# One layer of a hybrid attention / gated DeltaNet trunk: the later tiles of the input projection issued in another order

## The chip, the cores and the metric

The kernel runs on one NeuronCore of a Trainium2 chip. The core has five engines with a queue each, and each queue is worked off in order: TensorE (PE in the profile; PEld is its weight load), VectorE (DVE), ScalarE (ACT), GpSimd (POOL) and SyncE (SP), which here issues the DMAs. The metric is device time in microseconds (us) from one launch, lower is better. Times below are from the hardware profiler or from the runs without it.

## The reference

A layer maps `x` of 1024 tokens by 1024 features to the same shape, in float32. Only the first of its three sub-layers (mixer, cross-attention to 256 memory tokens, SwiGLU) is touched:

```python
h = _rms_norm(x, g_mix_pre[l])
proj = h @ w_in[l]
aq, ak, av, dqkv, dgate, dalpha, dbeta = jnp.split(proj, IN_SPLITS, axis=-1)
aq = _rope(aq.reshape(b, s, ATTN_HEADS, ATTN_HEAD_DIM), positions)
ak = _rope(ak.reshape(b, s, ATTN_KV_HEADS, ATTN_HEAD_DIM), positions)
attn_o = _window_attention(aq, ak, av, attn_sink[l])            # +-128 tokens, 8 heads, 2 KV heads
dn_o = _gated_deltanet(dqkv, dgate, dalpha, dbeta, ...)         # 4 heads, two directions
mix = jnp.concatenate([attn_o, dn_o], axis=-1) @ w_out[l]
x = x + _rms_norm(mix, g_mix_post[l])
```

The DeltaNet part solves, in chunks, a unit lower triangular system for each head and direction and then scans over the chunks; at its end the output is multiplied by `silu(gate)`:

```python
sol = lax.linalg.triangular_solve(tmat, rhs, left_side=True, lower=True, unit_diagonal=True)
_, o = lax.scan(step, state0, xs)
o = o * jax.nn.silu(gate.astype(jnp.float32).reshape(b, s, DN_HEADS, DN_HEAD_V))
```

## The kernel before

Float32 products are built from a rounded high part and the rest (`split`, lines 102 and 103: ACT casts, DVE or POOL subtracts), three matmuls for each product. The normalised input `hT` stays in SBUF, transposed, in two halves of 512 tokens. A tile of the input projection is 128 of the 2832 columns: `load_w` (line 125 issues the DMA) loads and splits its weights, `proj` takes two PSUM banks from the pool `pg` (three banks), and `gemm_b` (line 260) does 24 matmuls of 512 columns for each half. "Half tile" below means these 24 matmuls.

The program issues tiles and other steps by three lists. A letter is a kind of step, a digit its tile or head:

- `ORDER_1`: D (projection and convolution of a DeltaNet head's q, k, v), P (prep: chunk products for a head), B (`base_inverse` for two heads: a forward substitution of 32 by 32 blocks, 30 rounds of two DVE operations at lines 510 and 512, begun by line 501 and ended by line 514; it reads `d_u` from DRAM at line 495 and stores to `d_inv` at line 519).
- `ORDER_2`, the one that is edited: G (`gate_proj`: ACT evicts each half with Silu, line 736, and SP stores it to `d_gate`, line 737), L (`levels` of a head: fetches the base inverses at line 530, copies at 540 to 553, then builds the inverse of the whole chunk from PE products at 569 and 575, with short DVE and ACT operations between, and stores it at 594), A (`attn_proj`: DVE evicts each half twice, lines 709 and 710, four DMAs rotate it, line 714, POOL adds, line 715, SP stores to `d_q` or `d_k`, line 716), V (`value_proj`, tile to `d_v`), W (`next_windows`: starts two attention windows and finishes the ones before).
- `ORDER_3`: M (memory norm), s01 (a step of both scans), W, K and V (keys and values of the memory). The scans' PE products are at line 763; they need the levels of all heads, and in their second half the gates, loaded from `d_gate`. Key products are at 891, value products at 907.

There are 16 windows (8 token blocks for 2 KV heads). One loads `kr`, `qr` and `vr`, splits them (lines 616 to 625, ACT and POOL), multiplies scores (633), reduces them on DVE (635), takes Exp on ACT (642 and 646), scales (650), transposes on PE (656), splits, and multiplies by the values (661). `kr`, `qr`, `vr` and the value bank have one buffer each.

What order do the engines run? The lists are not the queue order. A scheduler that plays the program through on a model of time (`schedule_with_timeline_sim=True`) deals out the instructions to the engines: of those that are ready in its model, the one that the program issues first goes first; weight loads go 300 places ahead (`AHEAD`). The result is fixed when the kernel is compiled, and the engines then keep to it. So an entry of a list sets a step's priority, and steps of later entries fill what earlier ones leave free.

After the scans come the output projection (`mid_gemm`, PE at line 991), cross-attention and the feed-forward part (from line 1072 on), which the lists do not touch.

Of the kernel before, what the change touches and what calls it, by code (L numbers as in the profile page):

```python
# [33 lines left out]


ORDER_1 = "D0 P0 D1 P1 D2 P2 D3 P3 B0 B1".split()
ORDER_2 = "G0 G1 G2 G3 L0 L1 V A4 A0 A1 W L2 L3 W W A2 A3 W".split()
ORDER_3 = ("M " + "s01 W K " * 5 + "s01 K " * 3 + "s01 V V").split()


# [35 lines left out]
def tile_hybrid_block(  # L76
# [11 lines left out]
    if dump is None:  # L88
        def dump(name, ap):
            pass  # L90
# [597 lines left out]
    def issue(order, table):  # L688
        for o in order:
            table[o[0]](*(int(c) for c in o[1:]))  # L690
# [47 lines left out]

    issue(ORDER_2, {"A": attn_proj, "V": value_proj, "G": gate_proj, "L": levels, "W": next_windows})
    dump("d_q", d_q); dump("d_k", d_k); dump("d_gate", d_gate); dump("d_v", d_v)  # L740
# [752 lines left out]
```

## Time and profile before

| what | value |
|---|---|
| median of 3 runs | 1596.54 us (1593.78 to 1598.5) |
| the profiled execution | 1601.45 us |
| its span, first to last instruction | 1599.7 us |
| mean granted clock of TensorE | 0.983 |
| stretch from the first gate tile to the output projection | 211.67 to 607.84 us |

The profiled execution is one run, with its own time; 1.75 us of it lie outside the span. In the profile a line `L260 PE MATMUL pg<-hhi,whi` is a matmul issued by line 260 of the kernel that writes the tile `pg` from `hhi` and `whi`. A wait row reads: engine, tile and line that waited, what released it, then the sum in us, how often, the longest. In a timeline row the first two numbers are start and duration. A busy share near one says that an engine had something in work, not that it worked at its full rate: the granted clock stands beside it.

### The profile page before, as it was taken

Reading aid. Unit: us, or ns where it says so; the run is one execution under the profiler, and the core shown is the slowest. Engines: PE = TensorE matmul, PEld = TensorE weight load, DVE = VectorE, ACT = ScalarE, POOL = GpSimd, SP = SyncE. Lnnn points to the kernel's source line nnn. Section 1 sums busy time; section 2 is a strip of 40 time slices with the busy share of each in tenths; the row PEclk is TensorE's granted clock in tenths of the full one; section 3 lists DMA queues with packets and bytes.
Section 4 is the critical chain, followed back from the end, with each engine's and each line's share of the span. In section 5 each row is a group of like instructions: output and inputs, shape, how many; then the busy total and the mean of one; then the engine's idle time right before and its main releaser. Section 6 shows DMA issues by size and latency. Waiting matters only on the chain. (4 is left out here: it accounts for less than half of the span.)

```text
span 1599.7 us, 21414 instructions
## 1 busy us (share of the span) xinstructions
PE 1523.6 (95%) x7558; PEld 1274.7 (80%) x7558; DVE 1034.0 (65%) x1596; ACT 766.2 (48%) x1561; POOL 522.8 (33%) x479
## 2 busy tenths in 40 slices
PE   6999889988899989999999999999999999999998
PEld 5877778877799967788888777778888888888786
DVE  6846886967677765454345549778765555587575
ACT  6566543326957785564334566223322323344532
POOL 2367653234335610243301140335433433100021
PEclk9999999998999999999999999999999999999999
DMA  6134258474999675354222254444333333763344
GB/s 205 41 109 124 59 159 239 129 192 122 296 324 277 193 266 191 145 185 152 73 69 80 90 185 139 150 157 152 100 120 118 104 99 99 272 222 108 110 169 160
DMA packets 265400, 247.29 MB, mean 155 GB/s; under 512 B 43960, under 2 KB 200525, under 8 KB 265293
## 3 DMA queue, kind: packets, MB, share of 16 engines
q1 hardware_dynamic: 265293, 245.93, 48.7%
q8 instruction: 59, 0.97, 0.3%
q14 instruction: 48, 0.39, 0.1%
HBM read 175.86 MB, written 67.40 MB: 152 GB/s over the span
## 5 line engine op out<-in xcount | busy, mean ns | idle before, releaser
L102 ACT CAST whi<-wraw 128x1024 fp32r<-128x1024 f32 x108 | 113.3, 1050 | 147.7 <-PE pA L1166 34.5
L103 POOL TENSOR_TENSOR wlo<-wraw,whi 128x1024 fp32r<-128x1024 f32 x48 | 118.4, 2467 | 165.2 <-ACT whi L102 150.8
L260 PE MATMUL pg<-hhi,whi 128*128 128x512 f32 x352 | 141.5, 403 | 0.0
L260 PE MATMUL pg<-hlo,whi 128*128 128x512 f32 x352 | 140.8, 401 | 0.0
L260 PE MATMUL pg<-hhi,wlo 128*128 128x512 f32 x352 | 140.8, 400 | 0.0
L103 DVE TENSOR_TENSOR wlo<-wraw,whi 128x1024 fp32r<-128x1024 f32 x60 | 75.5, 1260 | 86.0 <-ACT whi L102 76.5
L991 PE MATMUL pmg<-whi,b 128*128 128x512 f32 x384 | 120.0, 400 | 2.6 <-ACT whi L102 2.2
L1166 PE MATMUL pA<-s,whi 128*128 128x512 f32 x352 | 109.7, 393 | 1.4 <-ACT m L1183 1.4
L285 DVE SCALAR_TENSOR_TENSOR acc<-cp,cols,acc 128x1024 f32<-128x1024 f32 x48 | 77.8, 1622 | 34.8 <-ACT acc L283 34.1
L991 PEld LDWEIGHTS pmg<-whi,b 128*128 128x128 f32 x384 | 72.3, 191 | 18.2 <-ACT whi L102 2.7
L1243 POOL TENSOR_TENSOR act<-act,up 128x512 f32<-128x512 f32 x33 | 48.2, 1460 | 103.9 <-DVE up L1242 46.1
L260 PEld LDWEIGHTS pg<-hhi,wlo 128*128 128x128 f32 x352 | 67.5, 192 | 13.3
L260 PEld LDWEIGHTS pg<-hhi,whi 128*128 128x128 f32 x352 | 67.6, 192 | 13.2 <-ACT hhi L102 0.3
L260 PEld LDWEIGHTS pg<-hlo,whi 128*128 128x128 f32 x352 | 67.4, 191 | 13.1
L1354 PE MATMUL pdX<-dhl,whi 128*128 128x512 f32 x264 | 76.1, 391 | 1.5 <-DVE zv L1409 0.8
L1166 PEld LDWEIGHTS pA<-s,whi 128*128 128x128 f32 x352 | 65.3, 188 | 15.2 <-ACT m L1183 2.0
L1384 POOL TENSOR_SCALAR frs<-sq 128x1 f32<-128x1 f32 x8 | 11.9, 1497 | 195.8 <-ACT jk L1373 194.9
L1215 POOL TENSOR_TENSOR sr<-wraw 128x512 f32<-128x512 f32 x22 | 29.0, 1318 | 134.1 <-DMA wraw<-in_w_gate_up_dram 120.9
L991 PE MATMUL pmg<-wlo,b 128*128 128x512 f32 x192 | 71.5, 392 | 0.0
L1166 PE MATMUL pA<-s,wlo 128*128 128x512 f32 x176 | 68.8, 392 | 1.6 <-DVE wlo L103 1.6
L102 ACT CAST whi<-araw 128x1024 fp32r<-128x1024 f32 (+1 forms) x36 | 35.4, 982 | 71.3 <-PE pdX L1354 27.6
L103 DVE TENSOR_TENSOR wlo<-araw,whi 128x1024 fp32r<-128x1024 f32 (+1 forms) x36 | 40.8, 1133 | 39.6 <-ACT whi L102 39.4
(411 smaller groups left out, 4272.5 us busy)
## 6 DMA issues: line engine op xcount, KB each, us to landing
wraw<-in_w_gate_up_dram SPq DMA_DIRECT2D x52, 512.0 KB, 4.1
kv<-d_kv SPq DMA_DIRECT2D x32, 512.0 KB, 6.9
wraw<-in_w_in_dram SPq DMA_DIRECT2D x22, 512.0 KB, 4.0
b<-in_w_down_dram SPq DMA_DIRECT2D x20, 512.0 KB, 5.9
araw<-d_as SPq DMA_DIRECT2D x20, 512.0 KB, 3.8
d_kv<-kv SPq DMA_DIRECT2D x8, 1024.0 KB, 6.3
pz<-d_pz SPq DMA_DIRECT2D x32, 256.0 KB, 6.6
wraw<-in_w_ckv_dram SPq DMA_DIRECT2D x16, 512.0 KB, 6.4
```

The costliest lines, as they stand in the source:

```text
L102: nc.scalar.copy(hi, src)
L103: (eng or nc.vector).tensor_tensor(lo, src, f32(hi), ALU.subtract)
L260: nc.tensor.matmul(p_, w[:, k, :], ah[a][:, k, :], start=(k == 0 and i == 0), stop=(k == nk - 1 and i == 2))
L285: nc.vector.scalar_tensor_tensor(acc, cp[:, t:t + S], taps[t], acc, ALU.mult, ALU.add)
L991: nc.tensor.matmul(pp[t], act[a][:, k, tt], w_[:, kk, :], start=(k == 0 and i == 0), stop=(k == KT - 1 and i == 2))
L1166: nc.tensor.matmul(out_, w[a][:, k, :], xx[b_][:, k, :], start=(start and k == 0 and i == 0), stop=(k == HK - 1 and i == 2), skip_group_ch ...
L1215: nc.gpsimd.tensor_tensor(s[0], b_[:, 0:HK], b_[:, HK:], ALU.add)
L1243: nc.gpsimd.tensor_tensor(o_, o_, up, ALU.mult)
L1354: nc.tensor.matmul(banks[t], a[:, k - k0, tt], w, start=(first and k == 0 and i == 0), stop=(k == NB - 1 and i == 2), skip_group_check=not ...
L1384: nc.gpsimd.tensor_scalar(rs, sq[:, 1, t:t + 1], sq[:, 0, t:t + 1], D * EPS, ALU.add, ALU.add)
```

## The change

One of the three lists is reordered. It has the same 18 entries.

```diff
 ORDER_1 = "D0 P0 D1 P1 D2 P2 D3 P3 B0 B1".split()
-ORDER_2 = "G0 G1 G2 G3 L0 L1 V A4 A0 A1 W L2 L3 W W A2 A3 W".split()
+ORDER_2 = "L0 L1 A4 V A0 A1 L2 L3 W W W G0 G1 G2 G3 W A2 A3".split()
 ORDER_3 = ("M " + "s01 W K " * 5 + "s01 K " * 3 + "s01 V V").split()
```

The levels of heads 0 and 1 come first, then the key tile (A4), the value tile, the query tiles of the first KV head (A0, A1), the levels of heads 2 and 3, and three pairs of windows. The four gate tiles, which stood at the front, follow these; the fourth pair of windows and the query tiles of the second KV head (A2, A3) are last. What each step does is the same.

## The prediction

> **What bounds the kernel now.** I read the page first, then busy times by stretch, then the order of single instructions at the edges of the stretches.
>
> ```profile
> span 1599.7 us, 21414 instructions
> PE 1523.6 (95%) x7558; PEld 1274.7 (80%) x7558; DVE 1034.0 (65%) x1596; ACT 766.2 (48%) x1561; POOL 522.8 (33%) x479
> PEclk9999999998999999999999999999999999999999
> ```
>
> TensorE (PE) is busy almost everywhere, so the total can fall only where PE waits, or works at a lower clock. The next table cuts the part that the change can reach (first gate tile to first matmul of the output projection) into stretches; columns are busy time (instructions) of PE, weight load, DVE, ACT, POOL, then granted clock, DMA share, GB/s.
>
> ```profile
> 211.67:255.70 44.03, 39.38 (x202) 33.15 (x200) 36.24 (x49) 24.16 (x61) 24.24 (x23) 0.96 0.62 168
> 255.70:345.58 89.88, 86.18 (x449) 72.54 (x448) 70.43 (x134) 25.86 (x59) 29.26 (x23) 0.98 0.66 172
> 345.58:375.70 30.12, 28.39 (x157) 24.65 (x156) 16.20 (x43) 14.65 (x41) 10.82 (x10) 0.94 0.53 144
> 375.70:430.00 54.30, 44.39 (x241) 36.97 (x240) 37.86 (x86) 40.68 (x107) 21.21 (x24) 0.81 0.68 215
> 430.00:567.09 137.09, 130.76 (x1015) 123.43 (x1014) 105.48 (x282) 100.17 (x284) 73.72 (x78) 1.00 0.86 262
> 567.09:607.84 40.75, 36.58 (x165) 29.38 (x164) 23.49 (x40) 30.58 (x61) 2.89 (x5) 0.92 0.78 266
> 607.84:1599.70 991.86, 968.49 (x4407) 797.93 (x4405) 596.18 (x790) 410.84 (x693) 247.92 (x195) 0.99 0.42 138
> ```
>
> The thin stretch is 375.7 to 430: the projections have run out, and PE has only levels and windows to do, whose steps wait for one another. Three of its slices, and what PE waited for between 376 and 430:
>
> ```profile
> 380.00:390.00 10.00, 7.36 (x45) 5.66 (x44) 9.37 (x16) 6.04 (x17) 6.74 (x6) 0.85 0.63 176
> 390.00:400.00 10.00, 9.42 (x40) 8.66 (x41) 5.70 (x16) 5.86 (x18) 1.47 (x2) 0.50 0.23 70
> 410.00:420.00 10.00, 8.68 (x43) 7.33 (x43) 5.77 (x16) 7.64 (x18) 3.77 (x6) 0.66 0.98 358
> PE pow L661 <- ACT ph L102: 3.7, 3, 2.0
> PE ptw L656 <- DVE m L635: 3.2, 2, 2.8
> ```
>
> No wait exceeds 2.8 us, but they come often and the clock falls to half for some microseconds: 390 to 400 looks 94% busy and does half the work.
> [...]
>
> Busy time counts overlapping matmuls twice, so I count **work**: each PE instruction at the spacing it has back to back.
>
> ```profile
> 344.00 0.39 PE L260 MATMUL pg<-hlo,whi 128*128 128x512 f32 x1
> 346.26 0.39 PE L260 MATMUL pg<-hhi,wlo 128*128 128x512 f32 x1
> 346.50 1.86 PE L569 MATMUL ps<-m,L 128*128 128x32 f32 x16
> 348.19 0.48 PE L260 MATMUL pg<-hhi,whi 128*128 128x512 f32 x1
> 403.06 0.34 PE L633 MATMUL psw<-klo,qs 128*128 128x384 f32 x1
> 403.41 0.33 PE L633 MATMUL psw<-klo,qs 128*128 128x384 f32 x1
> 424.75 0.60 PE L656 MATMUL ptw<-ident,sc 128*128 128x128 f32 x4
> 425.11 0.48 PE L661 MATMUL pow<-pl,vhi 128*128 128x512 f32 x1
> ```
>
> A 512-column matmul takes 2.26/10 = 0.226 us (ten of them lie from 344.00 to 346.26; I use 0.227); one of the two records of a plain float32 matmul 1.69/16 = 0.106 (0.108 used, 0.217 a matmul); a score matmul 0.174; a transpose 0.36/4 = 0.09. I take 0.115 for 256 columns. Summed over the order of instructions that each kernel compiles to, from the first gate tile on, and set against the time of the same instruction:
>
> ```profile
> 211.67 0.39 PE L260 MATMUL pg<-hhi,wlo 128*128 128x512 f32 x1
> 255.70 0.39 PE L260 MATMUL pg<-hhi,wlo 128*128 128x512 f32 x1
> 345.58 0.39 PE L260 MATMUL pg<-hhi,wlo 128*128 128x512 f32 x1
> 414.29 1.19 PE L763 MATMUL psc<-kv,pz 128*128 128x128 f32 x4 [0.36 <-DMA pz<-d_pz]
> 567.09 0.71 PE L907 MATMUL pcv<-whi,mT 128*128 128x512 f32 x2
> 607.84 0.63 PE L991 MATMUL pmg<-whi,s 128*128 128x512 f32 x2
> ```
>
> - 211.67 to 255.70: work 35.5, lost 8.5.
> - to 375.7 (last projection matmul): work 108.1 in 120.0, lost 11.9 (9.9%; 8.7% up to 345.58, 14% behind it).
> - to 414.29 (first scan matmul): work 18.8 in 38.6, lost **19.8** (51%).
> - to 432 (first key matmul): 12.6 in 17.7, lost 5.1.
> - to 567.09: 119.7 in 135.1, lost 15.4 (11.4%).
> - to 607.84: 31.1 in 40.75, lost 9.6.
>
> Together 325.8 of work, 70.3 lost.
>
> **The change part by part.** One line, the order of issue, is edited. No arithmetic, transfer or buffer is added or removed. In the compiled order the PE queue is the same up to 223 us and again from the output projection on, so 211.67 before and 991.86 behind stay. Between, the same instructions are dealt out anew:
>
> - *Levels and windows ahead, gates as filler.* The work done at the last projection matmul rises from 143.6 to 161.1, at the first scan matmul from 162.4 to 170.8; of the windows' 132 value matmuls (L661) about 20 are done by then, now 36. The first window's scores come at work 72.5 instead of 124.5. So the thin stretch, work 18.8, shrinks to 9.7. The gates, 8 half tiles of 24 matmuls, 43.6 us, now lie where windows wait.
> - *Attention tiles ahead of gates* under the second base inverse.
>
> ```profile
> L709 DVE TENSOR_TENSOR sn<-pg,sinT 128x512 f32<-128x512 f32 x10 | 6.9, 690 | 2.4 <-PE pg L260 2.3
> L710 DVE TENSOR_TENSOR rop<-pg,cosT 128x512 f32<-128x512 f32 x10 | 6.8, 680 | 0.0
> 231.97 2.07 DVE L514 TENSOR_TENSOR V<-A,bB 128x1024 f32<-128x1024 f32 x1
> 248.81 2.38 DVE L553 TENSOR_TENSOR D<-c,dmask 128x512 f32<-128x512 f32 x2
> 269.69 2.07 DVE L501 SCALAR_TENSOR_TENSOR A<-V,bB 64x1024 f32<-64x1024 f32 x1 [5.10 <-DMA V<-d_u]
> 318.73 2.05 DVE L514 TENSOR_TENSOR V<-A,bB 128x1024 f32<-128x1024 f32 x1
> 300.00:320.00 20.00, 18.78 (x95) 15.43 (x94) 19.40 (x37) 3.77 (x11) 8.63 (x8) 0.91 0.58 164
> ```
>
>   A rotary half tile costs DVE 1.37 us where a gate half tile costs it nothing. By the compiled order DVE has 7.5 us more in front of the second inverse, of which the 5.1 us wait at 269.69 hides the larger part, and 53.2 instead of 48.5 us between its first and last operation. It ends at 318.73 + 2.05 = 320.8 now, so at 325.5 (4.7 more) to 333 (12.2 more). Levels 2 and 3 hang on it: their first product came at 346.50, 25.7 later, without PE waiting for it. In the new order it stands at work 108.6, about 211.67 + 108.6 + 16 = 336. After the first inverse (end 234.0) the copies for its levels were complete at 251.2, 17 us behind, so the stall is 325.5 + 17 - 336 = 6 us, 14 with the late end, none if the copies go faster. I take 3.
> - *Silu and Exp interleaved.* ACT now evicts gates between softmax steps.
>
> ```profile
> L736 ACT ACT_TABLE_LOAD x1 | 1.3, 1283 | 0.0
> L736 ACT ACTIVATE gt<-pg 128x512 f32<-128x512 f32 x8 | 4.8, 595 | 9.9 <-PE pg L260 9.8
> ACT qs L624 <- DMA qr<-d_q: 13.2, 3, 8.9
> ACT khi L616 <- DMA kr<-d_k: 10.5, 4, 4.7
> ```
>
>   The compiled order has two table loads from the first gate to the last window, and eight after: 6 x 1.28 = 7.7 us of ACT, which is 29 to 75% busy in the stretches from 255.7 to 430, spread over 100 us. I cost it at nothing for PE; without that cover it is 7.7. The last two rows are ACT's longest waits between 300 and 414 (sum, times, longest); they matter below.
>   [...]
> - *DMAs.* The eight gate stores move behind window loads on SP's queue, the rotary copies ahead. A store behind a late Silu holds back the window loads after it. It gets no term of its own: it is part of the loss rate of the mixed stretch, whose bounds in the sum, 8% and 16%, are 13 us apart.
>
> The sum of what is lost: 8.5 as before; 125.6 of work up to the last projection at 9.9%, 13.8 (bounds 8%, 10.9, and 16%, 24); the stall 3; the thin rest, 9.7 of work at 51% would be 10, at the mixed rate 1, and I take 8 since it is windows alone again; 8.9 of work at the scan's start at 29%, 3.6; 117.4 at 11.4%, 15.1; 29.2 at the end at 24%, 9.1. That is 61.1 on 326.3 of work, against 70.3 on 325.8: 9 us less. I round up to 10, since windows' loads move out of the scan, where the DMA share is 0.86. The profiled execution took 1601.45 (1.75 around its span), 4.9 above the median of 1596.54; 10 off gives 1591.5 for it and **1586** for the median.
>
> **The rivals.**
> 1. *Full mixing* (0.22): the thin stretch goes wholly and the scan stays denser. Lost 8.5 + 10.9 + 1 + 3 + 12 + 8 = 43, 27 won, 1570. For it: 430 to 567 runs at full clock with windows mixed in. Against it: DVE is at 70 of 90 us from 255.7 to 345.6, and a window's chain does not get shorter.
> 2. *The second inverse is late* (0.17): a stall of 12 instead of 3 with the half clock behind it; PE's queue is in order, so gates and windows stand behind it. The gain is used up: 1591 to 1600, within 0.3%. For it: DVE is 97% busy from 300 to 320. Against it: 25.7 us of room now.
> 3. *ACT's queue blocks the gates* (0.25, the slower side): casts of window loads wait for DMA at ACT (13.2 + 10.5 us before the scan), and now stand in front of gate evictions and weight casts. With three PSUM buffers for half tiles, PE runs dry once an eviction is later than one half tile, 24 x 0.227 = 5.4 us. With 7.7 of table loads that is 31 us. Above 10 us landing on PE the change loses; at two thirds, 21, it is 11 slower: 1607. For it: ACT is strictly in order. Against it: the weights are loaded well ahead.
> 4. *The change moves nothing that matters* is excluded by the compiled order: levels start 14 us of work earlier, windows 52.
>
> **How the numbers follow.** My forecast has 0.36. About 0.3% (4.8 us) is what a measurement of this kernel tells from no change. Faster by more: rival 1 and 0.9 of my own, with a little of rival 3's light end: 0.56. Slower: most of rival 3: 0.23. Within: 0.21. The range goes from rival 1 to rival 3, 1569 to 1606; my case alone is 1578 to 1592.
>
> **What would show it.** Right: no slice at clock 0.50 between 375 and 430; the last projection later than 375.7, near 400; the first scan matmul near 418 with levels finished; the output projection starting 10 us before 607.84; eight table loads. Wrong: PE waits on L569 behind DVE or ACT copies of levels 2 and 3 over 5 us (rival 2), or PE waiting at L260 for a released `pg` bank or a late `whi` over 10 us in sum (rival 3); a difference behind 607.84 would overturn the whole account.

## The result, and the profile after

The changed kernel is slower: 1610.16 us (median of 5 runs, 1608.47 to 1614.96) beside 1598.5 us for the kernel before in the same job (5 runs, 1593.78 to 1605.71), a ratio of 1.0075 with a 95% interval of 1.0049 to 1.0100. The forecast was 10 us faster. The page of the changed kernel, lines as shown of before:

```profile
span 1608.4 us, 21407 instructions
PE 1520.2 (95%) x7558; PEld 1273.9 (79%) x7558; DVE 1040.8 (65%) x1596; ACT 775.2 (48%) x1567; POOL 524.0 (33%) x479
PEclk9999999899999999999999999999999999999999
```

Shares and mean clock tell nothing: TensorE is 95% busy in both, and from the first gate tile's place to the output projection's start its granted clock is 0.95 in both. The table by stretches does (columns as before: busy time and count of PE, weight load, DVE, ACT, POOL, then granted clock, DMA share, GB/s):

```profile
209.87:256.04 46.17, 40.73 (x202) 33.37 (x200) 36.68 (x51) 21.36 (x58) 25.97 (x24) 0.93 0.58 150
256.04:320.00 63.96, 54.79 (x280) 46.19 (x279) 55.17 (x98) 19.29 (x41) 24.81 (x21) 0.92 0.70 188
320.00:382.62 62.62, 58.27 (x309) 49.54 (x308) 47.21 (x100) 44.95 (x106) 21.30 (x18) 0.95 0.58 152
382.62:411.70 29.08, 29.08 (x172) 25.51 (x171) 16.29 (x44) 17.19 (x47) 10.37 (x11) 1.00 0.40 110
411.70:430.94 19.24, 12.28 (x57) 9.32 (x56) 12.35 (x24) 15.25 (x35) 10.31 (x12) 0.86 0.69 220
430.94:572.73 141.79, 137.39 (x1065) 131.39 (x1064) 106.64 (x287) 99.75 (x284) 69.12 (x76) 0.98 0.88 275
572.73:607.85 35.12, 31.77 (x147) 26.30 (x146) 20.33 (x32) 25.67 (x48) 0.94 (x2) 0.95 0.90 296
607.85:616.40 8.55, 0.39 (x2) 0.00 (x0) 4.89 (x5) 4.77 (x6) 0.00 (x0) 0.81 0.98 346
616.40:1608.40 992.00, 968.97 (x4404) 798.44 (x4404) 593.80 (x786) 407.53 (x687) 248.39 (x195) 0.99 0.41 136
```

Read it from below. Behind the output projection's start nothing changed: 992.00 against 991.86 (that they agree so closely is partly luck, as the other kernels will show). That start came at 616.40 instead of 607.84, 8.6 later. Two stretches are new in kind: 256 to 320, where PE is busy 86% at clock 0.92 (before, 255.7 to 345.6 was 96% at 0.98) and DVE 86%, and 607.85 to 616.40, where PE does all but nothing. In front of the scan the hole has closed as far as the change could close it: 382.6 to 411.7 has PE busy throughout at full clock.

Counted as the prediction counts, each PE instruction at its back-to-back spacing, the losses are as follows. Half tiles of the projection are numbered from 0; the 20 that the second order issues are 24 to 43. (The expectations further down call them projection tiles.)

| stretch, by the same count of projection matmuls, then by the same kind of product | lost before | forecast | lost after |
|---|---|---|---|
| half tiles 24 to 29 | 8.5 | 8.5 | 10.7 |
| 29 to 34 | 0.4 | } 16.8 with the stall | **11.2** |
| 34 to the last projection matmul | 11.5 | } | **16.2** |
| to the first scan matmul (the thin stretch) | 19.8 | 8 | 12.0 |
| to the first key matmul | 5.1 | 3.6 | 1.7 |
| to the first value matmul | 15.4 | 15.1 | 13.8 |
| to the output projection | 9.6 | 9.1 | **14.5** |
| sum | 70.3 | 61.1 | 80.1 |

The three rows from the thin stretch to the first value matmul won 12.8 us, where the forecast had 13.6. The rows in bold gave back 20.4: 15.5 between half tile 29 and the last projection matmul, 4.9 at the end; the first row gave another 2.2.

**The first hole, at 281 us.** Four excerpts of the changed kernel's timeline (start, duration, then the instruction; in brackets the idle time before it and what ended it): ACT, DVE, PE, and two windows over it.

```profile
271.30 0.28 ACT L580 ACTIVATE z<-ps 128x128 f32<-128x128 f32 x1 [2.31 <-PE ps L575]
280.62 0.41 ACT L586 COPY mov<-Z 64x256 f32<-64x256 f32 x1 [7.46 <-DVE Z L583]
```

```profile
274.17 2.06 DVE L501 SCALAR_TENSOR_TENSOR A<-V,bB 64x1024 f32<-64x1024 f32 x1 [3.62 <-DMA V<-d_u]
276.26 1.22 DVE L503 SCALAR_TENSOR_TENSOR A<-V,bB 64x1024 f32<-64x1024 f32 x1
277.52 0.69 DVE L710 TENSOR_TENSOR rop<-pg,cosT 128x512 f32<-128x512 f32 x1
278.12 1.23 DVE L553 TENSOR_TENSOR D<-c,dmask 128x512 f32<-128x512 f32 x1
279.37 0.30 DVE L581 STREAM_TRANSPOSE D<-z 32x128 f32<-32x128 f32 x1
...
283.68 0.69 DVE L709 TENSOR_TENSOR sn<-pg,sinT 128x512 f32<-128x512 f32 x1
284.29 0.70 DVE L510 TENSOR_TENSOR tmpb<-A 128x30 f32<-128x30 f32 x1
285.02 0.96 DVE L587 COPY mov<-Z 64x256 f32<-64x256 f32 x2
```

```profile
285.93 3.65 PE L569 MATMUL ps<-mov,L 128*128 128x64 f32 x16 [5.03 <-DVE mov L587]
...
289.91 0.63 PE L260 MATMUL pg<-hhi,whi 128*128 128x512 f32 x1
```

```profile
280.00:286.00 6.00, 0.97 (x5) 0.50 (x4) 5.79 (x11) 2.37 (x5) 3.14 (x4) 0.96 0.40 131
286.00:292.00 6.00, 6.00 (x22) 5.46 (x23) 5.74 (x15) 0.75 (x2) 1.28 (x1) 0.50 0.34 85
```

These are steps of the levels of head 0. The input of its short steps (written by L580) is there at 271.58. L581, the first of them, starts at 279.37, 7.8 later. Nothing that it needs is late (the mask in front of it, at 278.12, is for the next head): it stands in DVE's queue behind L501, the second inverse's first operation, which waits for its own DMA until 274.17 (2.6 us of the 7.8), then behind L501 and L503 (3.3), a rotary eviction (0.6) and a mask (1.2). PE's queue is in order as well: its next product, L569, waits 5.03 us for `mov`, with projection matmuls standing behind it. Then it runs at half clock: 0.50 granted from 286 to 292, and a projection matmul lasts 0.63 us instead of 0.39. Before, DVE stood before the same L501 even longer, 5.10 us, and PE did not notice: it had gate half tiles to do, which need nothing from DVE, and its first level product came at 278.6, when L501 was done.

Here the granted clock is 1.00 up to 285 and 0.50 from 286 on, behind a gap of 5.03 us; in the kernel before it fell from 1.00 (386 to 387) to 0.50 (388 to 390) with no wait of PE over 1.99 us from 375.7 to 387. What sets the clock is not shown.

**The largest row, half tile 34 to the last projection matmul.** It has no single hole. Two windows, and what PE waited for most between 255 and 412 beside the 5.03 us (sum, times, longest):

```profile
304.00:320.00 16.00, 13.24 (x70) 11.08 (x69) 15.73 (x31) 5.59 (x11) 6.39 (x6) 0.89 0.55 153
350.00:360.00 10.00, 7.78 (x47) 7.11 (x47) 9.85 (x13) 6.45 (x14) 7.79 (x6) 0.86 0.87 204
PE ps L569 <- DVE L L562: 2.6, 2, 1.4
PE ps L560 <- DVE Z L592: 1.8, 2, 0.9
```

DVE is 98% busy in both windows, in the first with the rounds of the inverse, which ends at 336.1, and PE waits up to 1.5 us at a time for short steps of the levels, at a clock below one (0.89 and 0.86). What the rounds have to do with it is tried below.

**The second hole, at 608 us.** PE and ACT of the changed kernel:

```profile
607.85 0.39 PE L907 MATMUL pcv<-wlo,mT 128*128 128x512 f32 x1
616.40 1.22 PE L991 MATMUL pmg<-whi,s 128*128 128x512 f32 x2 [8.17 <-ACT vv L911]
```

```profile
607.37 0.59 ACT L911 COPY vv<-pcv 128x512 f32<-128x512 f32 x1
610.93 1.04 ACT L102 CAST whi<-wraw 128x1024 fp32r<-128x1024 f32 x1 [2.98 <-DMA wraw<-in_w_out_dram]
612.17 1.04 ACT L102 CAST b<-b 128x1024 fp32r<-128x1024 f32 x1 [0.19 <-DMA b<-d_mix]
613.52 1.04 ACT L102 CAST b<-b 128x1024 fp32r<-128x1024 f32 x1 [0.31 <-DMA b<-d_mix]
614.82 1.04 ACT L102 CAST b<-b 128x1024 fp32r<-128x1024 f32 x1 [0.25 <-DMA b<-d_mix]
615.77 0.58 ACT L911 COPY vv<-pcv 128x512 f32<-128x512 f32 x1
```

The last product of the values ends at about 608.2. Its eviction, 0.58 us of work, comes at 615.77: `vv` has one buffer, filled at 607.37 by the eviction before, whose store has to empty it; and the compiled order of ACT puts a weight cast and three casts of `b` between the two evictions, each of which waits for a DMA. In the kernel before (ACT) the last L911 stands ahead of the `b` casts:

```profile
607.35 0.60 ACT L911 COPY vv<-pcv 128x512 f32<-128x512 f32 x1
...
619.26 1.06 ACT L102 CAST b<-b 128x1024 fp32r<-128x1024 f32 x1 [0.45 <-DMA b<-d_mix]
```

### The profile page after: what moved, and what is told of

Its sections match the earlier page's. It is cut to its first block, busy times and chain, and to the rows that moved or that the text cites. A ratio compares the mean times of both kernels' runs of the same rounds, so it can differ in the third digit from the quotient of the medians.

```text
span 1608.4 us, 21407 instructions
## 1 busy us (share of the span) xinstructions
PE 1520.2 (95%) x7558; PEld 1273.9 (79%) x7558; DVE 1040.8 (65%) x1596; ACT 775.2 (48%) x1567; POOL 524.0 (33%) x479
## 5 line engine op out<-in xcount | busy, mean ns | idle before, releaser
L260 PE MATMUL pg<-hhi,whi 128*128 128x512 f32 x352 | 142.0, 404 | 0.0
L260 PE MATMUL pg<-hhi,wlo 128*128 128x512 f32 x352 | 142.0, 404 | 0.0
L260 PE MATMUL pg<-hlo,whi 128*128 128x512 f32 x352 | 141.0, 401 | 0.0
L260 PEld LDWEIGHTS pg<-hhi,whi 128*128 128x128 f32 x352 | 68.2, 194 | 13.6 <-ACT hhi L102 0.3
L260 PEld LDWEIGHTS pg<-hhi,wlo 128*128 128x128 f32 x352 | 68.2, 194 | 13.4
L260 PEld LDWEIGHTS pg<-hlo,whi 128*128 128x128 f32 x352 | 68.0, 193 | 13.5
L1166 PEld LDWEIGHTS pA<-s,whi 128*128 128x128 f32 x352 | 65.3, 188 | 15.1 <-ACT m L1183 2.0
```

The costliest lines, as they stand in the source:

```text
L260: nc.tensor.matmul(p_, w[:, k, :], ah[a][:, k, :], start=(k == 0 and i == 0), stop=(k == nk - 1 and i == 2))
L1166: nc.tensor.matmul(out_, w[a][:, k, :], xx[b_][:, k, :], start=(start and k == 0 and i == 0), stop=(k == HK - 1 and i == 2), skip_group_ch ...
```

## The experiments

Ratios are against the kernel before on the same chip, from 5 rounds each. Losses come from one profile a kernel and scatter by 2 to 5 us in a stretch; verdicts rest on them only where a ratio agrees. Behind the output projection's start, where the work is the same, the profiles take 986 to 995 us (`h2_g3_late_A`, which has some window work left there, 999). And where an edit leaves work out or changes a list, the scheduler deals out the rest anew, so such a run prices the work together with the order that goes with it; `e1`, `e2` and `f1` keep the changed kernel's order up to the end.

**The end.** Two buffers for `vv` (`e1_vv2`), one of the key eviction's two given up for the space:

```diff
-        cv = mk.tile([P, ML], F32, tag="cv", name="cv", bufs=2)
+        cv = mk.tile([P, ML], F32, tag="cv", name="cv", bufs=1)
-            vv = mk.tile([P, 512], F32, tag="vv", name="vv", bufs=1)
+            vv = mk.tile([P, 512], F32, tag="vv", name="vv", bufs=2)
```

> The changed kernel with two buffers for the tile vv (and one instead of two for cv, to make room). The compiled queues are the same up to the value products; only the last value eviction (L911) now stands ahead of the casts of b on ACT. Theory E (the end: the output projection waited 8.2 us for that eviction, which stood behind three casts that wait for d_mix loads): 8 us less than the changed kernel, ratio to before 1.002 to 1.003, first L991 matmul near 608, no wait of PE on L911. Rival (that wait only takes up slack, the next loads are late anyway): ratio stays 1.006 to 1.009 and the wait shows at the next operand.

Measured 1610.65 us, 1.0069 (1.0048 to 1.0090). The end's loss fell from 14.5 to 10.9 and PE's wait on L911 from 8.2 to 3.8, not to nothing: one `b` cast and a weight cast that waits 4.63 us for its DMA still stand ahead of the last eviction. The scan lost 3 more (16.9 instead of 13.8), so in sum nothing. The missing key buffer is not shown to be the reason: from the first key to the first value product `e1` took 134.3 us, the changed kernel 131.2, and `e2` below, with the buffers of `e1`, 129.7. The next edit takes no buffer away: the last eviction goes out in two halves through the key buffers, free by then (`f1_end`; alone on the kernel before, `g4_before_end`).

```diff
-            vv = mk.tile([P, 512], F32, tag="vv", name="vv", bufs=1)
-            nc.scalar.copy(vv, pp[t])
-            nc.sync.dma_start(d_mv[t, :, ch * 512:(ch + 1) * 512], vv)
+            for i, (n, m) in enumerate([("cv", ML)] * 2 if ch + t == 2 else [("vv", 512)]):
+                vv = mk.tile([P, m], F32, tag=n, name="vv", bufs=512 // m); nc.scalar.copy(vv, pp[t][:, i * m:(i + 1) * m])
+                nc.sync.dma_start(d_mv[t, :, ch * 512 + i * m:ch * 512 + (i + 1) * m], vv)
```

> The changed kernel with the last value eviction written through the two cv buffers, idle by then, instead of vv (one more ACT copy and one more store of 128 KB); cv and vv keep their sizes, every queue is the same up to there. e1_vv2 had one cv buffer less, which may have cost the scan what the end gave. Theory E: PE's wait on L911 goes from 8.2 to under 1 us and the kernel is 5 to 8 us faster than the changed one: ratio 1.002 to 1.004. Rival (slack): ratio 1.006 to 1.009, with another wait in its place at the output projection.

> The kernel before with the end edit alone: the control for f1. Theory (the edit only cures a wait that the changed kernel's ScalarE order brought): before's ScalarE has the last value eviction ahead of the three b casts already and waits 1 us on it, so 0.999 to 1.001. Rival (the edit is a gain of its own for any order): 0.995 to 0.997, and then f1's 6 us are not a cost of the change.

`f1_end`: 1603.74 us, 1.0017 (1.0004 to 1.0031), 0.58% below the change alone. Its timeline, ACT and PE:

```profile
608.61 1.05 ACT L102 CAST whi<-wraw 128x1024 fp32r<-128x1024 f32 x1 [1.48 <-DMA wraw<-in_w_out_dram]
609.68 1.14 ACT L911 COPY vv<-pcv 128x512 f32<-128x512 f32 x3
```

```profile
609.52 0.39 PE L907 MATMUL pcv<-wlo,mT 128*128 128x512 f32 x1
610.87 0.72 PE L991 MATMUL pmg<-whi,s 128*128 128x512 f32 x2 [0.96 <-ACT vv L911]
```

L911 now follows the products at once, PE waits 0.96 instead of 8.17, and the end's loss is 7.5. `g4_before_end`: 1597.45 us, 0.9981 (0.9965 to 0.9998). The edit is thus worth a little in the old order too, 0.2%; 0.4% of the 0.58%, some 6 us, is what the change itself broke at the end. The trace's own difference there, 14.5 against 9.6, says 5. The 0.2% is at the edge of what can be told: it lies between the two expectations, and the medians with and without the edit, 1597.45 and 1597.72, are level. That PE's wait fell with the eviction's place is the firmer evidence.

**The table loads.** `e1_vv2` with the gates evicted by a plain copy; Silu is left out.

```diff
-            nc.scalar.activation(gt, pp[hf], AF.Silu)
+            nc.scalar.copy(gt, pp[hf])
```

> e1_vv2 with the gate evicted by a plain copy, so that the gate's Silu is left out; the seven table loads between the gates and the windows go, all other queues are the same instruction for instruction. Theory A (ACT's queue: table loads and what waits behind them cost the mixed stretch its time): 6 to 9 us less than e1_vv2, ratio near 0.996. Theory D (VectorE bounds 256 to 320, levels wait behind the second base inverse there): within 2 us of e1_vv2; the 5 us wait of L569 on L587 stays.

Measured 1609.43 us, 1.0064 (1.0044 to 1.0084), as `e1_vv2` (1.0069). The changed kernel does load tables eight times for gates and windows, as forecast (ACT's groups: busy us, mean ns, idle time before):

```profile
L736 ACT ACT_TABLE_LOAD x4 | 5.1, 1283 | 0.1
L642 ACT ACT_TABLE_LOAD x3 | 3.8, 1283 | 0.1
L646 ACT ACT_TABLE_LOAD x1 | 1.3, 1283 | 0.0
```

They cost nothing that a measurement of this size finds (each interval reaches 0.2%, 3 us, to either side; the 7.7 us of the six added loads would be 0.5%).

**The second inverse on DVE.** First only its 30 rounds left out for heads 2 and 3, in the changed kernel (`f2_noinv_after`) and in the kernel before (`f3_noinv_before`):

```diff
-        for j in range(1, 31):
+        for j in range(1, 31 if g == 0 else 1):
```

> The changed kernel with the 30 rounds of the second base inverse left out (27 us of VectorE work; heads 2 and 3 get a wrong inverse). Theory D: the loss between P29 and P39 falls from 26 to 8 to 12 us and the kernel is 12 to 18 us faster than the changed one: ratio 0.996 to 1.000. Rival W (the windows' own chain and DMA loads stop PE there, VectorE is only busy): 2 to 6 us faster, ratio 1.004 or more.

> The kernel before with the same 30 rounds left out. Theory D: VectorE's load is covered by gate work there, so 0 to 5 us faster, ratio 0.997 to 1.000, and f2_noinv_after is level with it or faster. Rival W: the same gain in both, f2 stays 8 to 12 us slower than f3.

1603.17 us, 1.0015 (0.9999 to 1.0031), against 1601.37 us, 0.9999 (0.9982 to 1.0015). The rounds, with the order that goes with them, cost the changed kernel 0.6%, about 10 us, and the kernel before nothing; 12 to 18 us had been expected. By the traces they sit between half tiles 34 and 39, whose loss fell from 14.5 to 5.5. The five half tiles ahead kept theirs, 11.2 as with the rounds: L501 and a wait that the profile puts down to a DMA are still in the queue (`f2_noinv_after`, DVE), and PE still waited 5.2 us for L587.

```profile
277.11 2.06 DVE L501 SCALAR_TENSOR_TENSOR A<-V,bB 64x1024 f32<-64x1024 f32 x1 [4.38 <-DMA d_v<-vt]
...
282.30 0.30 DVE L581 STREAM_TRANSPOSE D<-z 32x128 f32<-32x128 f32 x1
```

So next the inverse stays whole, but is issued later, and DVE's compiled order has L581 to L587 of the first levels ahead of L501 (`g1_blate`, with the end edit):

```diff
-ORDER_1 = "D0 P0 D1 P1 D2 P2 D3 P3 B0 B1".split()
-ORDER_2 = "L0 L1 A4 V A0 A1 L2 L3 W W W G0 G1 G2 G3 W A2 A3".split()
+ORDER_1 = "D0 P0 D1 P1 D2 P2 D3 P3 B0".split()
+ORDER_2 = "L0 L1 A4 V A0 B1 A1 L2 L3 W W W G0 G1 G2 G3 W A2 A3".split()
-    issue(ORDER_2, {..., "W": next_windows})
+    issue(ORDER_2, {..., "W": next_windows, "B": base_inverse})
```

> The changed kernel with the end edit of f1 (1.0017), and the second base inverse issued later: B1 leaves the end of the first order and stands behind A0 in the second, so that in VectorE's compiled order its first operation (L501, which waits for V<-d_u) comes behind the short steps L581 to L587 of levels 0 and 1 instead of ahead of them. Theory (VectorE's queue is held by L501's wait and TensorE's levels stand behind it): the wait of L569 on mov L587 (5 us) goes or falls under 2 us, the stretch from the 29th to the 34th projection tile loses 2 to 5 us instead of 11 to 12, ratio about 0.996 to 0.999. Rival (the levels are late for their own inputs, whatever stands in VectorE's queue): the wait stays at 5 us and the ratio at 1.002. Second rival (the stall only moves): the stretch recovers but levels 2 and 3 wait for an inverse that ends later, the next stretch loses 6 us or more above its 13, ratio 1.000 to 1.003.

Measured 1610.85 us, 1.0077 (1.0056 to 1.0099), 0.6% worse than `f1_end`: a clear miss. The wait that the edit aimed at went from 5.5 us to 0.9, and another took its place (DVE, then PE):

```profile
281.70 2.06 DVE L501 SCALAR_TENSOR_TENSOR A<-V,bB 64x1024 f32<-64x1024 f32 x1 [1.88 <-DMA V<-d_u]
...
295.23 0.43 DVE L592 TENSOR_SCALAR Z<-ps 64x256 f32<-64x256 f32 x1
```

```profile
295.72 0.66 PE L560 MATMUL ps<-ident,Ul 128*128 128x128 f32 x4 [3.25 <-DVE Z L592]
```

L592, the levels' last short step, now stands behind the inverse's first rounds. The stretch still lost 9.4 us, and the scan 22.4 where `f1_end` lost 13.9. The stall moved, but not to where the second rival put it: the inverse ended no later than in `f1_end` (334.3 against 336.6), and the stretch behind half tile 34 lost no more. What the scan's 8.5 come from is not shown.

Does the inverse carry the whole loss of these half tiles, then, or would anything do? For that all its DVE work, and with it its POOL work, was left out for heads 2 and 3, and zeros stored in its place (the lines from L501 on are three higher in these two), in the changed kernel with the end edit and in the kernel before with the end edit (excerpt, indentation left as it was):

```diff
+        if g:
+            nc.gpsimd.memset(A, 0.0)
+        else:
             nc.vector.scalar_tensor_tensor(A[0:64], V[0:64].rearrange("p r s -> p s r"), -1.0,
...
-                                  (A if i == d else V)[64 * d:64 * d + 64])
+                                  (A if i == d or g else V)[64 * d:64 * d + 64])
```

> The changed kernel with the end edit of f1, and for heads 2 and 3 the whole second base inverse left out on VectorE (L501, L503, its 30 rounds and L514; zeros are stored in its place), so neither the wait for V<-d_u nor the rounds stand in VectorE's queue; loads and stores of the inverse stay. Theory (the inverse's place in VectorE's queue is all of the loss): the stretch from the 29th to the 34th projection tile loses under 3 us instead of 11 to 12 and the next 6 or less, so 15 us or more below f1's 1.0017: ratio 0.990 to 0.993. Rival (too little other TensorE work between the dependent steps of levels 0 and 1): the first stretch still loses 7 us or more, as f2's and g1's did, ratio 0.996 to 0.999.

> Control for h1: the kernel before with the end edit, and the same VectorE work of the second base inverse left out. Theory: before's gate tiles cover both the wait and the rounds, so no more than 2 us below the kernel before with the end edit (0.998): 0.996 to 0.999. Rival (that work costs in any order): 0.990 to 0.994, and h1's gain is then no cost of the change.

Measured 1597.35 us, 0.9972 (0.9952 to 0.9993), and 1603.89 us, 1.0015 (0.9998 to 1.0032). Without the inverse the changed order wins 0.45% over `f1_end`; the kernel before wins nothing (1.0015 against 0.9981 with the end edit alone, slower than either expectation). But it stays short of the theory's 0.990 to 0.993, and half tiles 29 to 34 still lose 8.2: the rival's figures. The wait that stood behind L501 is gone, though: head 0's product on `mov` starts at 277.9, 10 us earlier than in `f1_end`, with no wait of PE. The hole comes later, with another owner (`h1_noB1_after`, ACT, then PE):

```profile
291.75 0.40 ACT L619 CAST khi<-kr 128x256 fp32r<-128x256 f32 x1 [8.75 <-DMA vr<-d_v]
292.06 0.37 ACT L594 ACTIVATE Z<-ps 64x256 f32<-64x256 f32 x1
```

```profile
292.95 1.12 PE L563 MATMUL ps<-ident,Ul 128*128 128x128 f32 x4 [3.50 <-DVE Z L595]
```

Here it is ACT's queue: a window's cast comes after 8.75 us in which ACT waits for window loads, the levels' L594 stands behind it, L595 on DVE waits for L594, and PE for L595. Here, with one operation behind a late DMA taken away, the next one held the levels up.

**How many gate tiles lie ahead of the levels.** Only the second order is edited (`e3` and `e4` on top of `e1_vv2`, `f4` without an end edit, the others with that of `f1_end`):

```text
 e3_gsplit, g2_split_end:  "G0 G1 L0 L1 A4 V A0 A1 L2 L3 W W W G2 G3 W A2 A3"
 g3_split_blate:           "G0 G1 L0 L1 A4 B1 V A0 A1 L2 L3 W W W G2 G3 W A2 A3"
 h2_g3_late_A:             "G0 G1 G2 L0 L1 A4 V A0 A1 L2 L3 W W W G3 W A2 A3"
 h3_g3_late_B:             "G0 G1 G2 L0 L1 V A4 A0 A1 W L2 L3 W W G3 A2 A3 W"
 e4_gfirst, f4_gfirst:     "G0 G1 G2 G3 L0 L1 A4 V A0 A1 L2 L3 W W W W A2 A3"
```

> e1_vv2 with two gate tiles in front of the levels and two behind the third pair of windows. Theory D: while the second inverse runs PE has 21.8 us of gate work that needs no VectorE, so the loss between 256 and 320 falls by 4 to 8 us against the changed kernel; half of the filler for the windows stays; ratio 0.994 to 0.999. Theory A: five of eight table loads remain between first gate and last window by the compiled order, so 2 to 4 us less than e1_vv2 at most, ratio 1.000. Neither: same as e1_vv2.

> e1_vv2 with all four gate tiles in front again, levels, windows and attention tiles in the new order behind them. Theory D: the loss between 256 and 320 is that of before (about 6 us), but the thin stretch before the scan is back (first window scores at work 125 as before, lost about 20 us there); ratio 0.997 to 1.003. Theory A: two table loads, so no worse than before at all, 0.995 to 1.000, with the thin stretch not mattering.

> The order of e4 (gates in front, the rest as changed) with the buffers of the original, two cv and one vv. If the smaller cv cost e4 its scan (21 us lost there against 15 before): 4 to 6 us faster than e4, ratio 1.003 to 1.005. If not, 1.007 to 1.009, and the new order of levels, attention tiles and windows costs time by itself, gates in front or not.

> Gate tiles split (G0 G1 at the front, G2 G3 near the end) with the end edit of f1. Theory (the costs in the mixed stretch and at the end are separate): e3's 1.0024 had two value buffers, whose end wait cost 4 us still; with the end edit 0.998 to 1.001. Rival (the end edit helps only where all gates come last): 1.002 to 1.004.

> As g2, with B1 behind A4 in the second order, so that VectorE has the short steps of levels 0 and 1 ahead of L501. Theory: 4 to 8 us less than g2, ratio 0.993 to 0.997, both kernels beaten. Rival (with two gate tiles in front the wait already runs under their matmuls, as in the kernel before): the same as g2 within 0.15%.

> Order G0 G1 G2 L0 L1 A4 V A0 A1 L2 L3 W W W G3 W A2 A3 with the end edit: only the fourth gate tile near the end, the rest of the changed kernel's order. Theory of too little other work: three gate tiles in front cover levels 0 and 1, and the thin stretch has one more tile than before: 0.994 to 0.998. Rival (the new order of levels, attention and windows costs by itself, as f4's 1.007 had it): 1.002 to 1.006.

> Order G0 G1 G2 L0 L1 V A4 A0 A1 W L2 L3 W W G3 A2 A3 W with the end edit: the kernel before with only the fourth gate tile moved near the end. Theory (one tile of 5.5 us in the thin stretch takes the place of idle time there, and three in front still cover the levels): 0.994 to 0.997. Rival (the tile leaves a hole in front as large as the one that it fills): 0.998 to 1.001, as the kernel before with the end edit alone (0.998).

| kernel | gate tiles ahead | lost 29 to 34 | 34 to last projection | thin stretch and scan's start | ratio (95%) |
|---|---|---|---|---|---|
| f1_end | 0 | 12.1 | 14.4 | 15.1 | 1.0017 (1.0004 to 1.0031) |
| e3_gsplit | 2 | 9.5 | 14.2 | 18.2 | 1.0024 (1.0010 to 1.0038) |
| g2_split_end | 2 | 7.2 | 15.6 | 16.2 | 1.0010 (0.9994 to 1.0026) |
| g3_split_blate | 2, inverse later | 4.0 | 20.1 | 12.1 | 1.0002 (0.9984 to 1.0019) |
| h2_g3_late_A | 3 | 4.8 | 15.3 | 19.8 | 0.9994 (0.9977 to 1.0011) |
| h3_g3_late_B | 3 | 2.3 | 18.2 | 15.6 | 1.0016 (0.9997 to 1.0035) |
| e4_gfirst | 4 | 0.7 | 17.5 | 24.6 | 1.0079 (1.0061 to 1.0097) |
| f4_gfirst | 4 | 0.4 | 18.0 | 24.9 | 1.0070 (1.0047 to 1.0092) |
| g4_before_end | 4, old order | 0.4 | 11.6 | 24.7 | 0.9981 (0.9965 to 0.9998) |

The third column falls as gate tiles go ahead of the levels, from 12 to 0.4; a later inverse takes 3 more off with two of them there. The fifth rises, by and large, as the gates leave the thin stretch. The fourth is larger in every new order than in the old. The gates are the cover in one place or in the other, and where they go decides only which hole is open. `e4` and `f4` show that the rest of the new order, with the gates left in front, is by itself 0.7% slower; 6 us of it lie in the fourth column and 2 in the scan by `f4`'s trace, the remainder is not located (its profiled execution, 1604.57 us, is 7 below its median). Of these seven expectations `f4`'s came out, and with `g2` the theory and with `g3` the rival; the ratios of `e3`, `e4`, `h2` and `h3` lie outside all that had been named. No order tried beats the kernel before by more than its interval; what does, barely, is the old order with the end edit, 0.9981 with level medians, and it beats the changed kernel by 0.9%.

## Why the prediction was wrong, step by step

- *"125.6 of work up to the last projection at 9.9%, 13.8 ... the stall 3."* This is the step that failed: 38.1 us lost from half tile 24 to the last projection matmul, where 25.3 was forecast, 27.4 of them behind half tile 29. The rate had been measured on a stretch in which the gates covered the levels, and was carried over to one from which the change takes them away. The upper bound of the rate, 24, with the stall of 3 would have come to 27, close to these 27.4.
- *The stall was looked for in the wrong place.* The prediction let levels 2 and 3 wait for the inverse's data. What waited were the levels of head 0 (and at 309 to 312, for 2.6 us, those of head 1), which need nothing of the second inverse, for their turn in DVE's queue behind it or between its rounds. The inverse ended at 336.1, later than the late end of 333, and yet the first product of levels 2 came at 349.7 with a wait of only 0.7 us: by then PE itself was late. The row of the 5.1 us wait was quoted in the prediction, and read as room that hides 7.5 us of DVE work. It was a place where DVE's queue stands still; it costs nothing only as long as nobody in need stands behind it.
- *The second inverse late* (rival 2): `f2` and `f3` price its rounds at 0.6% in the new order and nothing in the old. The rival had the engine and the stall of about 12 us, the wrong levels, and a sum within 0.3%, as it saw neither the loss at the end nor the rest of the loss behind half tile 34.
- *ACT's queue blocks the gates* (rival 3): by its own sign refuted. PE had no wait of note at L260 for a bank or a weight, and `e2` found the table loads worth nothing, as the sum had them. But ACT's strict order was the cause of the other loss, at a place that no rival named.
- *"29.2 at the end at 24%, 9.1"*: 14.5. The end was taken over as it was, since its instructions are the same. Their order on ACT is not: one compiled place for one eviction cost 5 to 6 us (`f1`, `g4`).
- *The thin stretch 8, the scan's start 3.6, the scan 15.1*: 12.0, 1.7 and 13.8, together 0.8 off, which is partly luck: misses of 4.0, 1.9 and 1.3 cancel. Levels and windows ahead, gates as filler did what was said. 382.6 to 411.7 runs at full clock and the scan's approach at 0.86, so the half clock left this place, as forecast (375 to 430 has 0.96, before 0.81). It is not gone but elsewhere, at 286 above all, since the whole part has 0.95 as before; the last projection matmul came at 411.4 instead of near 400 and the first scan matmul at 430.9 instead of near 418, both late by what was lost earlier.
- *Eight table loads* and *no difference behind the output projection's start*: right; the 0.14 us is closer than this stretch repeats (986 to 995).
- *"Busy time counts overlapping matmuls twice"*: a misreading that does no harm to the sum. An overlap counts once: 382.62 to 411.70 has 29.08 us busy with 172 instructions, though a projection matmul alone lasts 0.39. Busy time fails as a measure of work because it stays full at half clock: 286 to 292 has 6.00 of 6.00 us busy at 0.50.

The range, 1569 to 1606, ended 4 us below the measured 1610. It lacked a case that adds two losses on two engines' queues.

Left open: why the new order of levels, attention tiles and windows costs 0.7% with the gates in front; and how much of half tiles 24 to 29's 2.2 is scatter. The gains are not additive either: the rounds gave 0.6% without the end edit, the whole inverse 0.45% with it. With the end mended and the inverse left out, 0.28% (0.9972) is what is seen of the 10 us; that the rest would follow if no operation with a late DMA stood ahead of the levels was not tried.

## What to carry over

Before work that needs nothing from the other engines is moved away, ask what it hid: a rate of loss belongs to the mix of its stretch. Go through each in-order queue, not only that of the bounding engine, and mark the operations that wait for a DMA; whatever the new order puts behind them waits as well (L581 stood 7.8 us here, 2.6 of them for a DMA), and a single late short step stops the engine that sets the end (PE, 5.03 us). Where a scheduler fixes the order, read the places of the instructions at the end too, even if their code is untouched.

## What the runs showed of the hardware

A short DVE copy lasted five times as long while POOL added two tensors, 1.20 us instead of 0.22. The same copy of 32 by 128 in the changed kernel, and what POOL did meanwhile:

```profile
280.62 1.20 DVE L584 COPY Z<-z 32x128 f32<-32x128 f32 x1
283.43 0.22 DVE L584 COPY Z<-z 32x128 f32<-32x128 f32 x1
```

```profile
278.79 2.94 POOL L715 TENSOR_TENSOR rop<-rop,rot 128x512 f32<-128x512 f32 x2
284.23 0.72 POOL L617 TENSOR_TENSOR klo<-kr,khi 128x256 fp32r<-128x256 f32 x1 [2.49 <-ACT khi L616]
```

The slow copy ends at 281.82, 0.1 us behind POOL's 281.73; the fast one finds POOL idle. The profiles of the two kernels have 32 such copies (L583, L584): the 23 that find POOL idle take 0.22 us, 8 take 0.53 to 1.83 and each of these ends 0.1 us behind the end of a POOL operation, and one that starts 0.05 us ahead of POOL's takes 0.22. The transposes (L581, L582) took no longer there: the one at 279.37 runs under the first of POOL's two and takes 0.30 us, and all 10 of the two kernels that overlap one take 0.30 to 0.31, as the others do. In `h1_noB1_after`, where POOL is idle at this place, the copies take 0.22. The time lost lies in the chain of the first hole.
